# Rotary embeddings in a layer of a hybrid encoder: the last step on two engines, or as accumulating transfers into DRAM

## The chip, the cores and the metric

The kernel runs on one core of a Trainium2 chip. A core has five engines, each with its own instruction queue that it works through in order: TensorE (PE in the profile; PEld is its weight load), VectorE (DVE), ScalarE (ACT), GpSimd (POOL) and SyncE (SP). SP and POOL also issue the transfers (DMA) that move data between DRAM and the on-chip memory SBUF. Engines wait for one another and for transfers by semaphores. The metric is the device time of one execution in microseconds (us); smaller is better.

## The reference

One layer on 1024 tokens of width 1024, in float32: a feed-forward block, a token mixer and a second feed-forward block. The change is in the mixer. It multiplies the normalised input by one wide matrix whose columns are split into retention queries, keys, values and gates and the inputs of a neighbourhood attention:

```python
def _rotary(x, pos):
    half = x.shape[-1] // 2
    inv = 1.0 / (ROPE_BASE ** jnp.linspace(0.0, 1.0, half, dtype=jnp.float32))
    ang = pos[:, None] * inv[None, :]
    cos, sin = jnp.cos(ang), jnp.sin(ang)
    x1, x2 = x[..., :half], x[..., half:]
    return jnp.concatenate([x1 * cos - x2 * sin, x1 * sin + x2 * cos], axis=-1)
...
rq, rk, rv, rg, nq, nk, nv, g_ret, g_na = jnp.split(u @ w_in, points, axis=-1)
q = _rotary(heads(rq, RET_QK_DIM), pos)
k = _rotary(heads(rk, RET_QK_DIM), pos) * (RET_QK_DIM ** -0.5)
```

There are four retention heads of 128 channels. The queries and keys of a head, 128 x 1024 numbers each, are rotated: the first 64 channels of every token are mixed with the last 64.

## The kernel before

All products are formed with three matmuls on operands split into a high and a low part. `split` (L61, L62) makes them: ACT rounds a weight tile to the high part `wh`, DVE subtracts and so makes the low part `wl`. A matmul with `wl` (L90) can't start before DVE has done L62. The matmul lines are L88, L89 and L90.

The projections of the mixer are cut into jobs. One job yields two output tiles of 128 channels by 1024 tokens, by Winograd's scheme with seven products instead of eight (`Pairs.run`, L494 to L536). A product is a chain of twelve matmuls into one PSUM bank of 128 x 512. TensorE forms them in the order a11, s2, a12, s3, s1, a22, s4. DVE and ACT add the results into four quarters in SBUF: L509 (ACT), L514, L517, L524, L527, L528, L532 and L535 (DVE). The quarters are numbered j = 0 to 3; j // 2 says which of the two tiles, j % 2 which half of the tokens. They are finished in the order 0, 3, 1, 2, the first after the third product (L517), the second after the fifth (L527), then one after each of the last two (L532, L535). DVE also forms the next job's combined weights (L510, L511, L521, L530) and splits them.

When a quarter is done, `done(j)` handles it. Of the jobs around the change, four are rotary jobs (queries and keys of one head) and behind each stands a job of gates that ACT passes through silu (L1353); two jobs with a sigmoid follow. In a rotary job `rotate` (L1030 to L1033) turns each quarter in SBUF with four elementwise instructions: the two halves are multiplied crosswise with the sine table into a second tile `t`, the quarter is multiplied with the cosine table, and the two are added. Quarters 0 and 2 are turned by POOL, quarters 1 and 3 by DVE. Then `store` (L68) writes the quarter to DRAM from POOL's queue: to `rq` for queries, to `rk` for keys. They are read much later, by the retention.

Quarters and second tiles share six buffers of 128 x 512, named `ev`, and so do the quarters of the other jobs. A buffer is used again when its last reader is done, a store among them.

The order on each engine is not the order of the program. A scheduler lists the instructions engine by engine with its own estimate of times, picks a free buffer for each tile and puts in the waits. On the chip every engine keeps that order.

Of the kernel before, what the change touches and what calls it, by code (L numbers as in the profile page):

```python
# [13 lines left out]
ALU = mybir.AluOpType  # L14
# [1010 lines left out]
            nc.vector.tensor_scalar(q, q, RET_SCALE, None, ALU.mult)  # L1025


def rotate(eng, t, x, cos, sin):

    eng.tensor_tensor(t[0:64], x[64:128], sin[64:128], ALU.mult)  # L1030
    eng.tensor_tensor(t[64:128], x[0:64], sin[0:64], ALU.mult)
    eng.tensor_tensor(x, x, cos, ALU.mult)
    eng.tensor_tensor(x, x, t, ALU.add)  # L1033


def ret_cores(c, pool, spool, d, dec, fill, n):
# [157 lines left out]
def trunk_layer(ctx: ExitStack, tc, x, xt, g1a, w1i, w1o, g1b, gma, wmt, wnv, wrv, logits, dtab, rope, bias,  # L1194
                wro, wno, wmo, gmb, g2a, w2i, w2o, g2b, out):
    nc = tc.nc
# [5 lines left out]
    c = Core(tc, const, wpool, psum, dram)  # L1202
# [21 lines left out]
    def pool(stack, name, side="left"):  # L1224
        return stack.enter_context(tc.tile_pool(name=name, bufs=1, side=side, reuse_waits="tile"))
# [49 lines left out]
    def vproj(src, groups, done):  # L1275

        for toks in groups:
            banks = {t: c.bank() for t in toks}
            for k in range(KT):
                if k % 2 == 0:  # L1280
                    w = ahead.pop(k // 2) if k // 2 in ahead else c.load_w(src[k // 2])
                for t in toks:
                    tt = slice((t % 4) * P, (t % 4 + 1) * P)
                    c.mm3(banks[t], [q[:, k % 4, tt] for q in xh(t // 4, k // 4)], w[k % 2], k == 0, k == KT - 1)
                    yield
            for t in toks:
                done(t, banks[t])
# [32 lines left out]
    for f, k in zip(rest, FLIP_FILL):  # L1320
        fill(k)
        f = f()
# [5 lines left out]
    with tc.tile_pool(name="pa", bufs=1, reuse_waits="tile") as pa:  # L1328
        evpool[:] = [pa]
        fill.drain()  # L1330
        turners = (nc.gpsimd, nc.vector, nc.gpsimd, nc.vector)

        def half():
            return pa.tile([P, 512], F32, tag="ev", name="ev", bufs=6)

        tabs = [[pa.tile([P, 512], F32, tag="tab", name="tab", bufs=4) for _ in range(2)] for _ in range(2)]
        for h in range(2):
            for j in range(2):
                nc.sync.dma_start(tabs[h][j], rope[:, j, h * 512:(h + 1) * 512])

        for i, (_, _, f, g, fn) in enumerate(jobs):
            parts = {}

            def part(j):
                parts[j] = half()
                return parts[j]

            def done(j):
                h = j % 2
                if fn == "rotary":  # L1350
                    rotate(turners[j], half(), parts[j], *tabs[h])
                elif fn is not None:
                    nc.scalar.activation(parts[j], parts[j], fn)  # L1353
                c.store((f, g)[j // 2][:, h * 512:(h + 1) * 512], parts[j])
            mx.run(i, part, done)
            if i == 2:
                x1pool = pool(x1_stack, "x1b", "right")
                a21[:] = [x1pool.tile([P, 4, 512], F32R, name=f"a21{q}") for q in "hl"]
                for k in range(2):
                    raw = c.raw(d["a21"][:, 2 * k:2 * k + 2].rearrange("p k t -> p (k t)"))  # L1360
                    c.split(*[q[:, 2 * k:2 * k + 2].rearrange("p k t -> p (k t)") for q in a21], raw)
            if i == NHP - 1:
                for _ in vproj(wnv, ((4, 5, 6, 7),), done_nv):
                    pass
                for cb in range(4):
                    nc.sync.dma_start(d["nvg"][cb].rearrange("t (r c) d -> (t r) c d", r=4),
                                      d["nv"][:, KEY_OFF[cb]:KEY_OFF[cb] + 32, :])
# [216 lines left out]
```

## Time and profile before

| | |
|---|---|
| time, median of 3 runs | 2288.16 us (2287.96 to 2288.34) |
| the profiled execution | span 2285.9 us; 2.3 us below the median of the runs, which time what lies around the span too |
| TensorE busy | 2210.8 us, 97% |
| DVE busy | 1686.3 us, 74% |
| ACT busy | 1000.7 us, 44% |
| POOL busy | 650.9 us, 28% |
| the four rotary jobs with the gate jobs behind them | 814.9 to 978.9 us |

A row of a group names line, engine, operation, output and inputs, shape and count, then busy time in us, the mean of one in ns, and the idle time of the engine before it with what ended it. A row in order of time gives start, duration and, in brackets, the idle time before it. A wait row reads "who waited <- for whom: us in total, times, longest". A window row gives the busy time of each engine in a stretch (from:to), then the granted TensorE clock (1.00 is full speed), the share of the DMA engines' time and GB/s. Times within the execution count from the start of the span.

### The profile page before, as it was taken

To read this page: it belongs to the slowest core of one execution; us is meant where nothing else is said; L and a number is where in the kernel's file an instruction comes from. 1 tells how busy PE (TensorE), PEld (TensorE's weight loads), DVE (VectorE), ACT (ScalarE), POOL (GpSimd) and SP (SyncE) were. 2 spreads that over 40 slices of the span, in tenths; PEclk is the share of its full clock that TensorE was granted. 3 is DMA by queue.
4 is the path that set the end of the run, shared out by engine and by line. 5 is a ranking of instruction groups with operands and counts; after the bars stand their busy time and mean duration, and the time that the engine had idled before them with its cause. 6 is when DMAs were issued, how large, how long until landed. Compare 5 with 4: busy or idle time off the path is not lost. (4 is left out here: it accounts for less than half of the span.)

```text
span 2285.9 us, 30140 instructions
## 1 busy us (share of the span) xinstructions
PE 2210.8 (97%) x10232; PEld 1828.4 (80%) x10232; DVE 1686.3 (74%) x2928; ACT 1000.7 (44%) x2086; POOL 650.9 (28%) x779
## 2 busy tenths in 40 slices
PE   6899999999998999999999999999899999999998
PEld 5688888888787887778888888887578888888886
DVE  7998878755568667969876678537988888886444
ACT  5444434332344322259875665315544343433232
POOL 1121212169424133401101222101531212125942
PEclk9999999999999999999999999999999999999999
DMA  6353434597555452357754566766434444349865
GB/s 248 134 193 134 175 129 175 213 379 282 203 178 172 149 184 79 111 187 255 219 165 165 166 212 233 288 219 206 171 133 171 166 150 163 140 144 369 303 224 181
DMA packets 150090, 444.11 MB, mean 194 GB/s; under 512 B 18800, under 2 KB 46576, under 8 KB 147824
## 3 DMA queue, kind: packets, MB, share of 16 engines
q1 hardware_dynamic: 111216, 314.23, 40.2%
q0 software_dynamic: 38720, 127.96, 14.6%
q8 instruction: 81, 1.33, 0.2%
q14 instruction: 73, 0.60, 0.1%
HBM read 305.80 MB, written 140.51 MB: 195 GB/s over the span
## 5 line engine op out<-in xcount | busy, mean ns | idle before, releaser
L62 DVE TENSOR_TENSOR wl<-wraw,wh 128x512 fp32r<-128x512 f32 x512 | 363.9, 730 | 83.1 <-ACT wh L61 82.3
L61 ACT CAST wh<-wraw 128x512 fp32r<-128x512 f32 x516 | 297.9, 618 | 213.5 <-DVE wraw L530 63.8
L88 PE MATMUL ps<-wh,g 128*128 128x512 f32 x484 | 188.7, 390 | 0.0
L89 PE MATMUL ps<-wl,g 128*128 128x512 f32 x484 | 188.5, 389 | 0.0
L90 PE MATMUL ps<-wh,g 128*128 128x512 f32 x484 | 188.3, 389 | 0.0
L552 ACT ACTIVATE c<-c 128x512 f32<-128x512 f32 x88 | 55.5, 632 | 205.8 <-DVE c L517 105.8
L62 DVE TENSOR_TENSOR wl<-w,wh 128x512 fp32r<-128x512 f32 x77 | 75.5, 993 | 84.9 <-ACT wh L61 83.9
L62 DVE TENSOR_TENSOR wl<-x,wh 128x512 fp32r<-128x512 f32 x77 | 80.5, 1066 | 75.8 <-ACT wh L61 74.8
L61 ACT CAST wh<-t 128x512 fp32r<-128x512 f32 x58 | 36.0, 621 | 191.1 <-DVE t L511 191.0
L88 PE MATMUL ps<-a11h,wh 128*128 128x512 f32 x276 | 111.7, 405 | 7.5 <-ACT wh L61 7.3
L90 PE MATMUL ps<-a11h,wl 128*128 128x512 f32 x276 | 109.7, 398 | 5.0 <-DVE wl L62 4.9
L88 PE MATMUL ps<-a22h,wh 128*128 128x512 f32 x280 | 109.9, 392 | 0.0
L90 PE MATMUL ps<-a22h,wl 128*128 128x512 f32 x280 | 109.2, 390 | 0.6 <-DVE wl L62 0.6
L89 PE MATMUL ps<-a11l,wh 128*128 128x512 f32 x276 | 109.5, 397 | 0.1
L88 PE MATMUL ps<-a12h,wh 128*128 128x512 f32 x276 | 108.9, 394 | 0.3 <-ACT wh L61 0.3
L90 PE MATMUL ps<-a12h,wl 128*128 128x512 f32 x276 | 107.9, 391 | 1.3 <-DVE wl L62 1.3
L89 PE MATMUL ps<-a22l,wh 128*128 128x512 f32 x280 | 109.1, 390 | 0.0
L89 PE MATMUL ps<-a12l,wh 128*128 128x512 f32 x276 | 107.7, 390 | 0.0
L89 PEld LDWEIGHTS ps<-wl,g 128*128 128x128 f32 x484 | 90.9, 188 | 18.9 <-DVE wl L62 0.5
L90 PEld LDWEIGHTS ps<-wh,g 128*128 128x128 f32 x484 | 90.8, 188 | 18.9
L88 PEld LDWEIGHTS ps<-wh,g 128*128 128x128 f32 x484 | 90.8, 188 | 18.9
L68 POOL DMA_DIRECT2D g0a<-gth x33 | 18.0, 550 | 290.9 <-ACT gth L599 273.8
(435 smaller groups left out, 6540.1 us busy)
## 6 DMA issues: line engine op xcount, KB each, us to landing
wraw<-in_dram SPq DMA_DIRECT2D x218, 512.0 KB, 4.4
g<-g0s SPq DMA_DIRECT2D x44, 512.0 KB, 4.2
g<-g1s SPq DMA_DIRECT2D x44, 512.0 KB, 4.6
g<-g0a SPq DMA_DIRECT2D x33, 512.0 KB, 3.2
g<-g1a SPq DMA_DIRECT2D x33, 512.0 KB, 4.4
g0s<-gth POOLq DMA_DIRECT2D x44, 256.0 KB, 4.4
g0s<-cmb POOLq DMA_DIRECT2D x44, 256.0 KB, 3.7
g1s<-gth POOLq DMA_DIRECT2D x44, 256.0 KB, 4.5
```

What stands on the lines that cost most here:

```text
L61: self.done = [nc.scalar.copy(h, src).ins, (eng or nc.vector).tensor_tensor(l, src, hf, ALU.subtract).ins]
L62: (eng or nc.vector).tensor_tensor(l, src, hf, ALU.subtract).ins]
L68: self.nc.gpsimd.dma_start(dst, src)
L88: mm(ps, a[0], b[0], start=start, stop=False)
L89: mm(ps, a[0], b[1], start=False, stop=False)
L90: mm(ps, a[1], b[0], start=False, stop=stop)
L552: nc.scalar.activation(gate[j], gate[j], AF.Silu)
```

## The change

A quarter is no longer finished in SBUF. DVE makes two multiplications over all 128 channels: the second tile `t` is the quarter times the sine table, in its own place, and the quarter is multiplied with the cosine table. The quarter is stored so. Then two transfers from POOL's queue add `t` into the stored tile in DRAM, each 64 rows: the lower half of `t` onto the upper half of the tile and the other way round. Such an accumulating transfer must wait until the store before it has landed, and until it has itself landed the buffer of `t` is held. The program calls these transfers (`swaps`) when the next quarter is done. What is stored in the end is the same sum.

```diff
-def rotate(eng, t, x, cos, sin):
-
-    eng.tensor_tensor(t[0:64], x[64:128], sin[64:128], ALU.mult)
-    eng.tensor_tensor(t[64:128], x[0:64], sin[0:64], ALU.mult)
-    eng.tensor_tensor(x, x, cos, ALU.mult)
-    eng.tensor_tensor(x, x, t, ALU.add)
+def rotate(c, t, x, cos, sin, dst):
+
+    tt = c.nc.vector.tensor_tensor
+    tt(t, x, sin, ALU.mult)
+    tt(x, x, cos, ALU.mult)
+    c.store(dst, x)
+
+    def swap():
+        c.nc.gpsimd.dma_start(dst[0:64], t[64:128], accum_op=ALU.add)
+        c.nc.gpsimd.dma_start(dst[64:128], t[0:64], accum_op=ALU.add)
+    return swap
...
-        turners = (nc.gpsimd, nc.vector, nc.gpsimd, nc.vector)
+        swaps = []
...
             def done(j):
                 h = j % 2
+                dst = (f, g)[j // 2][:, h * 512:(h + 1) * 512]
+                while swaps:
+                    swaps.pop()()
                 if fn == "rotary":
-                    rotate(turners[j], half(), parts[j], *tabs[h])
-                elif fn is not None:
+                    swaps.append(rotate(c, half(), parts[j], *tabs[h], dst))
+                    return
+                if fn is not None:
                     nc.scalar.activation(parts[j], parts[j], fn)
-                c.store((f, g)[j // 2][:, h * 512:(h + 1) * 512], parts[j])
+                c.store(dst, parts[j])
```

In the changed kernel the lines below the function stand a few lower, and L1031 and L1032 are the two multiplications, L1036 and L1037 the two accumulating transfers. ACT, SP and TensorE keep their order; DVE and POOL change in the four rotary jobs alone.

The following rows show the order on an engine, as built: line, operation, output and inputs, shape, and what it waits for (DMASW0 to DMASW7 are the semaphores that POOL's transfers take in turn; a number behind a name tells tiles of one kind apart). First DVE in the second rotary job, from L528 to the first split of the gate job behind it. Before:

```order
L528 TENSOR_TENSOR ev_7125<-ps_7191,ev_7125 128x512
L1030 TENSOR_TENSOR ev_7211<-ev_7208,tab_6142 64x512 [waits DMASW5_49,DVE_49]
L1031 TENSOR_TENSOR ev_7211<-ev_7208,tab_6142 64x512
L1032 TENSOR_TENSOR ev_7208<-ev_7208,tab_6141 128x512 [waits DVE_49]
L532 TENSOR_TENSOR ev_7189<-ps_7218,ev_7189 128x512 [waits PE_49]
L1033 TENSOR_TENSOR ev_7208<-ev_7208,ev_7211 128x512 [waits DVE_49]
L1030 TENSOR_TENSOR ev_7236<-ev_7189,tab_6142 64x512 [waits DMASW2_49,DVE_49,Pool_49]
L1031 TENSOR_TENSOR ev_7236<-ev_7189,tab_6142 64x512
L535 TENSOR_TENSOR ev_7125<-ps_7242,ev_7125 128x512 [waits PE_49]
L1032 TENSOR_TENSOR ev_7189<-ev_7189,tab_6141 128x512 [waits DVE_49]
L1033 TENSOR_TENSOR ev_7189<-ev_7189,ev_7236 128x512 [waits DVE_49]
L62 TENSOR_TENSOR wl_7273<-wraw_7266,wh_7272 128x512 [waits DMAHW2_49,Activation_49]
```

And now:

```order
L528 TENSOR_TENSOR ev_7125<-ps_7189,ev_7125 128x512
L1031 TENSOR_TENSOR ev_7211<-ev_7206,tab_6142 128x512 [waits DMASW5_49,DVE_49]
L1032 TENSOR_TENSOR ev_7206<-ev_7206,tab_6141 128x512 [waits DVE_49]
L532 TENSOR_TENSOR ev_7187<-ps_7216,ev_7187 128x512 [waits PE_49]
L1031 TENSOR_TENSOR ev_7236<-ev_7187,tab_6142 128x512 [waits DMASW6_49,DVE_49]
L1032 TENSOR_TENSOR ev_7187<-ev_7187,tab_6141 128x512 [waits DVE_49]
L535 TENSOR_TENSOR ev_7125<-ps_7240,ev_7125 128x512 [waits PE_49]
L1031 TENSOR_TENSOR ev_7260<-ev_7125,tab_6140 128x512 [waits DMASW7_49,DMASW0_49,DVE_49]
L1032 TENSOR_TENSOR ev_7125<-ev_7125,tab_6139 128x512 [waits DVE_49]
L62 TENSOR_TENSOR wl_7271<-wraw_7264,wh_7270 128x512 [waits DMAHW2_49,Activation_49]
```

Six rows of rotation stand between L528 and L62 where eight stood. The first of the last two, which writes the second tile of quarter 2 (`ev_7260`), now waits for DMASW7 and DMASW0, the two accumulating transfers of quarter 0.

DVE in the first rotary job, from L527 on. Before:

```order
L527 TENSOR_TENSOR ev_6896<-ps_6879,ev_6877 128x512 [waits DMASW6_49,DMASW4_49,PE_49]
L528 TENSOR_TENSOR ev_6813<-ps_6879,ev_6813 128x512
L1030 TENSOR_TENSOR ev_6899<-ev_6896,tab_6142 64x512 [waits DMASW7_49,DMASW5_49,DVE_49]
L1031 TENSOR_TENSOR ev_6899<-ev_6896,tab_6142 64x512
L532 TENSOR_TENSOR ev_6877<-ps_6906,ev_6877 128x512 [waits PE_49]
L1032 TENSOR_TENSOR ev_6896<-ev_6896,tab_6141 128x512 [waits DVE_49]
L1030 TENSOR_TENSOR ev_6924<-ev_6877,tab_6142 64x512 [waits DMASW2_49,DVE_49,Pool_49]
L1033 TENSOR_TENSOR ev_6896<-ev_6896,ev_6899 128x512 [waits DVE_49]
L1031 TENSOR_TENSOR ev_6924<-ev_6877,tab_6142 64x512
L535 TENSOR_TENSOR ev_6813<-ps_6930,ev_6813 128x512 [waits PE_49]
L1032 TENSOR_TENSOR ev_6877<-ev_6877,tab_6141 128x512 [waits DVE_49]
L62 TENSOR_TENSOR wl_7001<-wraw_6954,wh_7000 128x512 [waits Activation_49]
```

And now:

```order
L527 TENSOR_TENSOR ev_6894<-ps_6877,ev_6875 128x512 [waits DMASW6_49,DMASW4_49,PE_49]
L528 TENSOR_TENSOR ev_6813<-ps_6877,ev_6813 128x512
L1031 TENSOR_TENSOR ev_6899<-ev_6894,tab_6142 128x512 [waits DMASW7_49,DMASW5_49,DVE_49]
L62 TENSOR_TENSOR wl_6999<-wraw_6952,wh_6998 128x512 [waits Activation_49]
L1032 TENSOR_TENSOR ev_6894<-ev_6894,tab_6141 128x512 [waits DVE_49]
L532 TENSOR_TENSOR ev_6875<-ps_6904,ev_6875 128x512 [waits PE_49]
L62 TENSOR_TENSOR wl_7022<-wraw_6954,wh_7021 128x512 [waits Activation_49]
L1031 TENSOR_TENSOR ev_6924<-ev_6875,tab_6142 128x512 [waits DMASW6_49,DVE_49]
L535 TENSOR_TENSOR ev_6813<-ps_6928,ev_6813 128x512 [waits PE_49]
L1032 TENSOR_TENSOR ev_6875<-ev_6875,tab_6141 128x512 [waits DVE_49]
L1031 TENSOR_TENSOR ev_6948<-ev_6813,tab_6140 128x512 [waits DMASW7_49,DMASW0_49,DVE_49]
L62 TENSOR_TENSOR wl_7041<-wraw_6952,wh_7040 128x512 [waits Activation_49]
```

The splits of the gate job's weights (L62) move forward: two of them stand ahead of the last two quarters' rotation and the third ahead of its last row, where the first stood behind seven rows of rotation. The quarter that POOL turned comes to DVE, with the wait for DMASW7 and DMASW0.

POOL in the second rotary job. Before:

```order
L1030 TENSOR_TENSOR ev_7165<-ev_7124,tab_6140 64x512 [waits DMASW2_49,DVE_49]
L1031 TENSOR_TENSOR ev_7165<-ev_7124,tab_6140 64x512
L1032 TENSOR_TENSOR ev_7124<-ev_7124,tab_6139 128x512 [waits DMASW0_49,Pool_49]
L1033 TENSOR_TENSOR ev_7124<-ev_7124,ev_7165 128x512 [waits Pool_49]
L68 DMA rq_99<-ev_7124 128x512 [waits Pool_49]
L68 DMA rk_100<-ev_7208 128x512 [waits DMASW7_49,DVE_49]
L1030 TENSOR_TENSOR ev_7260<-ev_7125,tab_6140 64x512 [waits DMASW6_49,DVE_49]
L1031 TENSOR_TENSOR ev_7260<-ev_7125,tab_6140 64x512
L1032 TENSOR_TENSOR ev_7125<-ev_7125,tab_6139 128x512 [waits DMASW1_49,Pool_49]
L68 DMA rq_99<-ev_7189 128x512 [waits DVE_49]
L1033 TENSOR_TENSOR ev_7125<-ev_7125,ev_7260 128x512 [waits Pool_49]
L68 DMA rk_100<-ev_7125 128x512 [waits Pool_49]
```

And now:

```order
L68 DMA rq_99<-ev_7124 128x512 [waits DMASW6_49,DVE_49]
L1036 DMA rq_99<-ev_7165 64x512 [waits DMASW7_49,DMASW6_49]
L1037 DMA rq_99<-ev_7165 64x512 [waits DMASW0_49]
L68 DMA rk_100<-ev_7206 128x512 [waits DMASW1_49,DVE_49]
L68 DMA rq_99<-ev_7187 128x512 [waits DMASW2_49,DVE_49]
L1036 DMA rk_100<-ev_7211 64x512 [waits DMASW3_49,DMASW1_49]
L1037 DMA rk_100<-ev_7211 64x512 [waits DMASW4_49]
L1036 DMA rq_99<-ev_7236 64x512 [waits DMASW5_49,DMASW2_49]
L1037 DMA rq_99<-ev_7236 64x512
L68 DMA rk_100<-ev_7125 128x512 [waits DMASW7_49,DVE_49]
L1036 DMA rk_100<-ev_7260 64x512 [waits DMASW7_49,DMASW0_49]
L1037 DMA rk_100<-ev_7260 64x512
```

The eight elementwise rows are gone, and behind each store come two rows L1036 and L1037, the first of which waits for that store to land. The stores of the later quarters stand behind them in the queue; quarter 1's store was put ahead of quarter 3's accumulations.

## The prediction

> **What bounds the kernel now.** I read the page's first part, then the stage that holds the change in windows, then who waited for whom there, then the engines in order of time.
>
> ```profile
> PE 2210.8 (97%) x10232; PEld 1828.4 (80%) x10232; DVE 1686.3 (74%) x2928; ACT 1000.7 (44%) x2086; POOL 650.9 (28%) x779
> ```
>
> TensorE is busy 97% of 2285.9 us, so an edit on other engines can only win stretches where TensorE waits. The four windows below run from the start of one L517 (product a12 added up in a rotary job) to the same line two jobs later: one rotary job and the silu job behind it, called a pair here.
>
> ```profile
> core 0: us, PE busy (x) PEld busy (x) DVE busy (x) ACT busy (x) POOL busy (x), PEclk, DMA share, GB/s
> 814.92:854.41 39.49, 38.67 (x169) 31.38 (x168) 33.64 (x44) 11.19 (x20) 16.73 (x16) 1.00 0.50 176
> 854.41:899.92 45.51, 40.62 (x169) 32.82 (x168) 32.83 (x45) 11.10 (x20) 15.69 (x16) 0.92 0.30 102
> 899.92:939.41 39.49, 38.67 (x169) 31.38 (x168) 34.24 (x45) 11.19 (x20) 16.77 (x16) 1.00 0.29 103
> 939.41:978.91 39.50, 38.69 (x169) 31.38 (x168) 34.23 (x45) 12.47 (x21) 16.77 (x16) 1.00 0.29 103
> ```
>
> Here are VectorE's (DVE's) instructions of the second pair, in order of time: start, duration, and the idle time before.
>
> ```profile
> 854.41 0.69 DVE L517 TENSOR_TENSOR ev<-ps,ev 128x512 f32<-128x512 f32 x1 [1.97 <-PE ps L90]
> 857.13 0.69 DVE L524 TENSOR_TENSOR ev<-ps,ev 128x512 f32<-128x512 f32 x1 [2.03 <-PE ps L90]
> 859.85 0.69 DVE L527 TENSOR_TENSOR ev<-ps,ev 128x512 f32<-128x512 f32 x1 [2.03 <-PE ps L90]
> 860.46 0.68 DVE L528 TENSOR_TENSOR ev<-ps,ev 128x512 f32<-128x512 f32 x1
> 861.15 0.69 DVE L1030 TENSOR_TENSOR ev<-ev,tab 64x512 f32<-64x512 f32 x1
> ...
> 867.23 1.64 DVE L1033 TENSOR_TENSOR ev<-ev 128x512 f32<-128x512 f32 x1
> 868.79 1.75 DVE L62 TENSOR_TENSOR wl<-wraw,wh 128x512 fp32r<-128x512 f32 x1
> ```
>
> L517, L524 and L527 each wait for one product of TensorE and stand 2.72 us apart, so a product costs 2.72 us and a pair of 14 products 38.08. The windows exceed that by 1.41, 7.43, 1.41 and 1.42 us, 11.67 in all. That is the most the change can win here. Who takes it:
>
> ```profile
> PE ps L90 <- DVE wl L62: 7.3, 7, 4.9
> ...
> 832.09 0.50 PE L90 MATMUL ps<-a12h,wl 128*128 128x512 f32 x1 [0.43 <-DVE wl L62]
> 835.49 0.50 PE L90 MATMUL ps<-s3h,wl 128*128 128x512 f32 x1 [0.39 <-DVE wl L62]
> ...
> 870.60 0.80 PE L90 MATMUL ps<-a11h,wl 128*128 128x512 f32 x1 [4.89 <-DVE wl L62]
> ```
>
> All of TensorE's idle time from 806 to 982 us has one cause: the low part `wl` of a weight tile of the next job, which DVE makes too late. In the first, third and fourth pair it is two short stalls, in the second one long one.
>
> **Why DVE is late.** First pair, DVE and then POOL in order of time, and last the group of the stage's eight L62 that split a computed tile `t` (count, busy us, mean ns, idle before):
>
> ```profile
> 830.25 1.79 DVE L62 TENSOR_TENSOR wl<-wraw,wh 128x512 fp32r<-128x512 f32 x1
> 831.96 1.77 DVE L1033 TENSOR_TENSOR ev<-ev 128x512 f32<-128x512 f32 x1
> 833.65 3.48 DVE L62 TENSOR_TENSOR wl<-wraw,wh 128x512 fp32r<-128x512 f32 x2
> ...
> 829.82 1.67 POOL L1030 TENSOR_TENSOR ev<-ev,tab 64x512 f32<-64x512 f32 x1 [0.67 <-DVE ev L535]
> ...
> L62 DVE TENSOR_TENSOR wl<-t,wh 128x512 fp32r<-128x512 f32 x8 | 5.5, 688 | 0.6
> ```
>
> While POOL rotates its second quarter (four instructions from 829.82 on), an L62 that takes 0.69 us elsewhere takes 1.74 to 1.79. Two DVE quarters of four instructions stand ahead of it.
>
> **The change part by part.**
>
> *Arithmetic.* Per rotary job before: two quarters of 4 instructions on DVE, two of 4 on POOL. After: four quarters of 2 on DVE, none on POOL. Half-height and full-height ones cost the same, by the rows of the stage:
>
> ```profile
> L1030 DVE TENSOR_TENSOR ev<-ev,tab 64x512 f32<-64x512 f32 x8 | 5.5, 687 | 0.2
> L1032 DVE TENSOR_TENSOR ev<-ev,tab 128x512 f32<-128x512 f32 x8 | 5.5, 683 | 0.0
> L1032 POOL TENSOR_TENSOR ev<-ev,tab 128x512 f32<-128x512 f32 x8 | 12.7, 1589 | 0.6
> L1033 POOL TENSOR_TENSOR ev<-ev 128x512 f32<-128x512 f32 x8 | 12.3, 1538 | 0.6
> L1030 POOL TENSOR_TENSOR ev<-ev,tab 64x512 f32<-64x512 f32 x8 | 11.8, 1472 | 24.7 <-DVE ev L517 21.3 <-DVE ev L535 3.4
> L1031 POOL TENSOR_TENSOR ev<-ev,tab 64x512 f32<-64x512 f32 x8 | 11.7, 1461 | 0.5
> ```
>
> So DVE's count stays at 8 a job, but two of them move to the first quarter, where DVE sat idle about 2 us per product (rows L524, L527), and the last three quarters cost 6 instructions in place of 8. POOL's 32 instructions (12.7 + 12.3 + 11.8 + 11.7 = 48.5 us) go, and with them the slowed DVE instructions.
>
> *First, third and fourth pair.* With 0.69 in place of 1.79, and two of the next job's three splits now standing ahead of the last two rotations (the order of the first pair above), the split for a12 is ready some 8 us before its matmul. The stalls go: 1.41 + 1.41 + 1.42 = 4.24 us.
>
> *Second pair.* Here all rotations still stand ahead of the split that TensorE waits for, so I walk the new order with the old pace: 0.61 us from start to start where an instruction doesn't need the one before, 0.70 where it does. L527 at 859.85, L528 860.46, the j3 quarter 861.15 and 861.76; L532 waits for the next product, 859.85 + 2.72 = 862.57; j1 quarter 863.25 and 863.95; L535 waits for the last product, 865.29; j2 quarter 865.98 and 866.6; L62 from 867.3 to 868.0, and TensorE goes on at 868.05 instead of 870.60: 2.55 us won. TensorE's last matmul ended at 870.60 - 4.89 = 865.71 and the next was due at about 865.55 (matmuls start 0.227 us apart, each shown for 0.39), so the loss falls from 5.05 to 2.5. The rest of the 7.43, 2.38 us, is the half clock that followed.
>
> *The clock.* Its rows: TensorE after idle stretches of about 3 us, and windows with the granted clock in the third column from the right.
>
> ```profile
> 730.28 0.47 PE L88 MATMUL ps<-s1h,wh 128*128 128x512 f32 x1 [3.02 <-DVE ev L520]
> 1022.63 0.44 PE L909 MATMUL ps<-k,qh 128*128 128x384 f32 x1 [2.51 <-ACT qh L64]
> 1613.03 1.22 PE L89 MATMUL ps<-wl,gh 128*128 128x512 f32 x2 [3.03 <-DVE wl L62]
> ...
> 726.00:734.00 8.00, 4.97 (x22) 3.80 (x21) 6.89 (x11) 3.63 (x8) 1.29 (x1) 1.00 0.38 131
> 1018.00:1026.00 8.00, 5.49 (x25) 4.15 (x24) 6.34 (x19) 5.29 (x11) 0.00 (x0) 1.00 0.97 274
> 1613.00:1623.00 10.00, 8.23 (x21) 5.21 (x21) 9.25 (x12) 3.04 (x6) 5.14 (x5) 0.51 0.46 158
> 869.00:875.00 6.00, 4.41 (x10) 3.31 (x11) 5.79 (x5) 0.84 (x2) 4.98 (x5) 0.50 0.13 48
> ```
>
> 4.89 us idle halved the clock, 2.51 didn't, and of two gaps of 3.0 one did. The forecast gap is 868.05 - 865.71 = 2.34, below the one that went free, so I take the 2.38 as won; lost, it is the lower end. The Trainium skill ("TensorE: Matmul & The Clock Gate", section "Why this matters for your kernels") wants no gaps over about 3 us, and says (section "Part 1: The HAM clock gate") that the window of 3.4 us is free-running. By that the sum is the same, the split pair of 3.0 us gaps agrees, and a gap of 2.34 wouldn't fill a window.
>
> *The transfers.* Added: 32 accumulating transfers of 64 rows (128 KB), on POOL's queue. Each first one of a quarter waits on POOL for its quarter's store to land; behind it stand later stores. The trace has none that accumulates. Nearest rows (issue, size, us to landing), and one store on POOL:
>
> ```profile
> 860.87 0.58 POOL L68 DMA_DIRECT2D rq<-ev  x1 [0.30 <-POOL ev L1033]
> ...
> rg<-rg SPq DMA_DIRECT2D x32, 128.0 KB, 2.5
> ...
> rq<-ev POOLq DMA_DIRECT2D x8, 256.0 KB, 2.3
> ...
> nvg<-nv SPq DMA_DIRECT2D x4, 9.3
> ...
> DMA to landing us min/median/max: 2.9/4.5/12.6
> ```
>
> An accumulation reads and writes DRAM: at least a store's 2.3 us, and at most the 12.6 of the slowest transfer on `nvg`, which is copied from DRAM to DRAM (median 9.3). I take a load and a store one after the other, 2.5 + 2.3 = 4.8, since these move tiles of this size between the same two places.
>
> Who needs them: six `ev` buffers serve four quarters and their products, so the j2 quarter's product reuses the j0 product's buffer (second pair's order: L1031 waits for DMASW7 and DMASW0). In the second pair j0 is done at 856.5, its store issues at 856.8 and lands at 859.1, the two accumulations issue at 859.4 and 860.0. DVE wants the buffer at 865.98: 6.0 us after the second issue, against 4.8. Hidden, with 1.2 to spare. In the first pair the same walk from L517 brings DVE to j2 at about 827, and the split behind it is wanted by the fifth product of the silu job, 814.92 + 8 x 2.72 + 0.45 = 837.1; so j2 may start as late as 835.7, while the second accumulation issues at about 820.5: 15.2 us of room. The silu job's own buffers wait for the j3 accumulations, issued near 828; their reader, L514, only frees PSUM, of which six banks stand ready. The load on POOL (12 transfers a job at 0.58) is less than the rotations that leave. ACT and SP keep their order; 8 MB more traffic in a stage whose DMA share is 0.29 to 0.50 costs nothing.
>
> *Sum.* 4.24 + 2.55 + 2.38 = 9.2 us of the profiled 2285.9. The three runs have a median of 2288.16, 2.3 us above that span; taking 9.2 off gives 2279.0. TensorE runs in order, so what follows moves with it.
>
> **Rivals.**
>
> *The clock drops all the same* after the 2.34 us gap: 2.38 given back, 2281.4. For it: one 3.03 gap that did. Against: 2.51 that didn't.
>
> *The two halves run one after the other*, 9.6 us from the first issue at 859.4 to 869.0. Then j2 starts 3.0 later, TensorE resumes at 871.05, 0.45 behind before, with the half clock: 4.24 - 0.45 = 3.8 won, 2284.4, no measurable change (0.2%, 4.6 us, is about what can be told from none). For it: nothing in the trace, which has no two halves of one tile. The Trainium skill ("DMA: Bandwidth & Descriptors", section "Rules for kernel authors") says that two transfers to disjoint partition halves serialize; no run here shows it.
>
> *Slower: the accumulation lands late and stands in front of TensorE.* Its place is the j2 quarter of the second pair: each us beyond 6.0 costs one, and soon the half clock's 2.38. At 12.8 us from issue the 9.2 less the clock's 2.4 are gone, at 15.2 the other three pairs start to lose too, and from some 16 the kernel is measurably slower. At 20 us: the second pair resumes at 882.05, 11.45 late, the others lose 20 - 15.2 - 1.41 = 3.4 each, in all 21.6, 2309.8. For it: 12.6 was seen on DRAM copies. Against: those moved under a DMA load that the second pair lacks (0.30).
>
> *Given back later:* the stretch of half clock at 1613 to 1623 follows a gap of 3.03 us and can shift with the earlier arrival. Up to 4 us either way (8.23 us of TensorE work at 0.51); 2283 or 2275.
>
> **How the numbers follow.** Forecast 0.60, clock drop 0.10, halves in turn 0.10, late landing 0.15, given back later 0.05. The range reaches from the forecast with 4 us won at 1613 (2275.0, rounded down to 2274.5) past the halves in turn to a landing at the seen 12.6 us (2279.0 + 6.6 + 2.4 = 2288.0); the lower bound of 2.3 us changes nothing, since 4.8 is hidden already. It leaves out most of the slower case and little else. Faster: forecast, clock drop and half of the last, 0.72; same: halves in turn and the rest, 0.13; slower 0.15.
>
> **What would show it.** Right: the four windows near 38.1, 40.6, 38.1, 38.1; all L62 near 0.69; TensorE idle in the stage once, for 2.3 us; accumulations landing in 3 to 6 us. Wrong: DVE idle ahead of L1031 with a DMA as the cause, a clock of 0.5 behind it, or POOL's stores of `rg` issued late.

## The result, and the profile after

The changed kernel takes 2281.1 us (median of 7 runs, 2278.7 to 2286.2), the kernel before 2288.3 on the same chip (7 runs, 2287.7 to 2293.4). The ratio is 0.9964, with a 95% interval of 0.9950 to 0.9977: 0.36% faster, 7.2 us by the medians and 8.2 by the ratio. The profiled execution took 2281.1 us; its span is 2279.3, 6.6 below that of before.

The page's first part and then the windows of the four pairs, from L517 to L517 as in the prediction (columns: TensorE, its weight load, DVE, ACT and POOL busy, granted clock, DMA share, GB/s):

```profile
PE 2209.3 (97%) x10232; PEld 1830.4 (80%) x10232; DVE 1662.9 (73%) x2928; ACT 1000.5 (44%) x2086; POOL 629.9 (28%) x779
```

```profile
818.39:856.47 38.08, 38.08 (x169) 31.53 (x168) 27.10 (x43) 11.09 (x20) 11.37 (x16) 1.00 0.73 206
856.47:897.42 40.95, 38.56 (x169) 31.37 (x168) 28.95 (x45) 11.10 (x20) 11.38 (x16) 1.00 0.52 143
897.42:935.50 38.08, 38.08 (x169) 31.53 (x168) 27.62 (x44) 11.21 (x20) 11.43 (x16) 1.00 0.50 138
935.50:973.58 38.08, 38.08 (x169) 31.53 (x168) 27.62 (x44) 12.49 (x21) 11.39 (x16) 1.00 0.52 139
```

Three pairs are at the 38.08 of pure TensorE work. The second keeps 2.87, at full clock. The four sum to 155.19 where they were 163.99: 8.80 won. Over the execution DVE has as many instructions as before (2928) and is busy 23.4 us less (1662.9, before 1686.3); in the stage it is 111.3 us where it was 134.9. TensorE's waits in the stage, then DVE in the second pair from the last product on, then DVE's split in the stage's groups:

```profile
PE ps L90 <- DVE wl L62: 2.4, 1, 2.4
```

```profile
867.35 0.69 DVE L535 TENSOR_TENSOR ev<-ps,ev 128x512 f32<-128x512 f32 x1 [0.57 <-PE ps L90]
868.08 0.69 DVE L1031 TENSOR_TENSOR ev<-ev,tab 128x512 f32<-128x512 f32 x1
868.80 0.69 DVE L1032 TENSOR_TENSOR ev<-ev,tab 128x512 f32<-128x512 f32 x1
869.41 0.69 DVE L62 TENSOR_TENSOR wl<-wraw,wh 128x512 fp32r<-128x512 f32 x1
...
L62 DVE TENSOR_TENSOR wl<-wraw,wh 128x512 fp32r<-128x512 f32 x54 | 35.5, 685 | 9.7 <-ACT wh L61 9.7
```

Of the seven stalls one is left. The j2 quarter's multiplication (868.08) has no idle time ahead of it, so the transfers that it must wait for had landed. Every L62 is at 0.69; before, the group of 49 had a mean of 908 ns.

The transfers, from the groups, DVE's waits and the DMA issues of the stage:

```profile
L1036 POOL DMA_DIRECT2D rq<-ev x8 | 7.0, 875 | 23.4 <-DMA rq<-ev 23.3
L1037 POOL DMA_DIRECT2D rq<-ev x8 | 9.2, 1154 | 0.0
...
DVE ev L1031 <- DMA rq<-ev: 5.4, 2, 3.4
DVE ev L514 <- DMA rk<-ev: 2.2, 2, 1.4
...
rq<-ev POOLq DMA_DIRECT2D x16, 128.0 KB, 4.3
rk<-ev POOLq DMA_DIRECT2D x16, 128.0 KB, 3.7
```

An accumulating transfer of 64 rows lands 3.7 to 4.3 us after its issue. DVE does wait for transfers, stores among them, 7.6 us in all, in the first and the fourth pair. None of it reaches TensorE.

Over the whole execution the stage gives 8.80 and the profile shows 6.6. The stage begins 3.47 later than before (818.39 against 814.92), although the orders of DVE and TensorE ahead of it are the same in both kernels; behind it 1.27 is won. Of the 3.47, 2.1 are there by 720 us and 1.4 come between 730 and 734, where the same gap of 3.0 us that went free before (730.28 in the prediction's rows) halved the clock:

```profile
732.38 0.77 PE L88 MATMUL ps<-s1h,wh 128*128 128x512 f32 x1 [3.00 <-DVE ev L520]
...
731.89:735.30 3.41, 2.92 (x7) 2.37 (x8) 3.27 (x6) 0.86 (x2) 0.00 (x0) 0.50 0.91 306
```

The 1.27 is the sum of several steps of both signs. In the profiles below the stage begins anywhere from 814.7 to 820.8, in no relation to the edits.

### The profile page after: what moved, and what is told of

Its sections match the earlier page's. It is cut to its first block, busy times and chain, and to the rows that moved or that the text cites. A ratio compares the mean times of both kernels' runs of the same rounds, so it can differ in the third digit from the quotient of the medians.

```text
span 2279.3 us, 30175 instructions
## 1 busy us (share of the span) xinstructions
PE 2209.3 (97%) x10232; PEld 1830.4 (80%) x10232; DVE 1662.9 (73%) x2928; ACT 1000.5 (44%) x2086; POOL 629.9 (28%) x779
## 5 line engine op out<-in xcount | busy, mean ns | idle before, releaser
L62 DVE TENSOR_TENSOR wl<-wraw,wh 128x512 fp32r<-128x512 f32 x512 | 353.3, 708 | 85.4 <-ACT wh L61 84.7
L62 DVE TENSOR_TENSOR wl<-w,wh 128x512 fp32r<-128x512 f32 x77 | 76.4, 1005 | 84.2 <-ACT wh L61 83.2
L62 DVE TENSOR_TENSOR wl<-x,wh 128x512 fp32r<-128x512 f32 x77 | 78.8, 1040 | 76.5 <-ACT wh L61 75.1
L88 PE MATMUL ps<-s2h,wh 128*128 128x512 f32 x232 | 91.8, 396 | 6.8 <-ACT wh L61 6.8
```

The costliest lines, as they stand in the source:

```text
L62: (eng or nc.vector).tensor_tensor(l, src, hf, ALU.subtract).ins]
L88: mm(ps, a[0], b[0], start=start, stop=False)
```

## Experiments

All windows are cut like the ones above; where a row of L517 slipped in DVE's order, work moves from one window to the next, so the sum of the stage is the surest column.

| | pair 1 | pair 2 | pair 3 | pair 4 | stage | TensorE's longest stall |
|---|---|---|---|---|---|---|
| before | 39.49 | 45.51 | 39.49 | 39.50 | 163.99 | 4.89 |
| changed | 38.08 | 40.95 | 38.08 | 38.08 | 155.19 | 2.39 |
| e1 POOL's quarters left out | 38.07 | 42.89 | 38.08 | 38.08 | 157.12 | 2.89 |
| e2 all on DVE | 39.32 | 46.62 | 39.33 | 39.33 | 164.60 | 5.77 |
| e3 no accumulation | 38.09 | 40.93 | 38.08 | 38.08 | 155.18 | 2.4 |
| e4 multiplied on POOL | 38.32 | 41.07 | 38.02 | 38.08 | 155.49 | 1.61 |
| e5 changed, again | 38.08 | 40.92 | 38.08 | 38.07 | 155.15 | 2.38 |
| e6 j2 one step later | 38.60 | 38.95 | 38.08 | 38.08 | 153.71 | 0.93 |
| e7 accumulated twice | 42.54 | 46.24 | 38.08 | 38.08 | 164.94 | 8.69 |
| e8 one transfer of 128 rows | 42.84 | 44.94 | 38.08 | 38.08 | 163.94 | 3.71 |
| e9 j0 twice | 39.25 | 45.80 | 38.08 | 38.08 | 161.21 | 5.16 |
| e10 j0 three times | 40.42 | 50.88 | 38.08 | 38.08 | 167.46 | 10.09 |

**Is it POOL's work beside DVE, or the number of DVE's instructions?** The theory: POOL's elementwise work slows DVE, and its removal is the whole gain. The rival: what counts is two instructions fewer ahead of the split. e1 takes POOL's work away and leaves the rest of the kernel before:

```diff
                 if fn == "rotary":
-                    rotate(turners[j], half(), parts[j], *tabs[h])
+                    if turners[j] is nc.vector:
+                        rotate(turners[j], half(), parts[j], *tabs[h])
```

> The kernel before, with the two quarters that POOL turns left unturned (their rotation is left out, they are stored as they are). DVE keeps its 8 rotation instructions a job, 4 a quarter, nothing accumulates in DRAM. Theory, contention: all the gain comes from POOL's elementwise work being gone from beside DVE. Walking the order of DVE's instructions from L517 on at 0.61 and 0.70 us, the split that TensorE waits for in the second pair is ready at the same place as in the changed kernel to within 0.1 us. Expected: the four pairs at 38.1, 41.0, 38.1, 38.1; one stall of TensorE in the stage, 2.4 to 2.5 us; every L62 near 0.69 us. Rival, count: the gain comes from DVE having two instructions fewer ahead of the split in the late quarters; then the pairs keep 39 to 39.5 and the second stays above 43. End to end the theory gives what the changed kernel has, about 2280 to 2282, the rival about 2286 to 2288.

Time 2281.3 us (10 runs), ratio to before 0.9961 (0.9947 to 0.9974). DVE's L535 in the second pair, TensorE's only stall in the stage, and a window of 2 us behind it:

```profile
867.91 0.69 DVE L535 TENSOR_TENSOR ev<-ps,ev 128x512 f32<-128x512 f32 x1
...
870.59 0.50 PE L90 MATMUL ps<-a11h,wl 128*128 128x512 f32 x1 [2.89 <-DVE wl L62]
...
872.50:874.50 2.00, 2.00 (x6) 1.56 (x5) 1.86 (x4) 2.00 (x5) 0.00 (x0) 0.50 0.00 0
```

DVE's order in the stage is that of the kernel before, instruction for instruction, and its busy time there is 112.1 us and not 134.9. Three pairs come to 38.08, so there the removal of POOL's work is enough by itself. In the second pair the theory falls short by 1.9 us. The split stands behind as many instructions after L535 as in the changed kernel, but L535 itself is no longer held by TensorE (no idle time in its row): the two more instructions ahead of it cost 0.50 us. That lengthened TensorE's gap from 2.39 to 2.89, and behind this one the clock halved: the other 1.44. So 6.87 of the 8.80 are POOL's work and 1.93 are the shorter order, most of that by way of the clock.

**What if DVE simply does it all?** e2 is the kernel before with one line changed:

```diff
-        turners = (nc.gpsimd, nc.vector, nc.gpsimd, nc.vector)
+        turners = (nc.vector,) * 4
```

> The kernel before with all four quarters turned on DVE in four instructions each, nothing on POOL and nothing accumulated: 16 rotation instructions a job in place of 8. Theory, contention plus place: without POOL beside it DVE has room in three pairs, which come to 38.1; in the second pair six rotation instructions and not two stand between L535 and the split that TensorE waits for, four more of about 0.62, so TensorE resumes 2.4 us later than in the changed kernel, a gap of 4.9 us, which halves the clock as the gap of 4.89 did before (2.4 more): second pair 45 to 46, stage about 160, so 5 longer than the changed kernel and 4 shorter than before. Rival, count: with twice the instructions on DVE all pairs grow past the kernel before, to 40 or more each.

Time 2292.7 us (10 runs), ratio to before 1.0021 (1.0007 to 1.0034): a little slower, where the theory had 4 us faster.

```profile
831.06 0.50 PE L90 MATMUL ps<-s2h,wl 128*128 128x512 f32 x1 [0.95 <-DVE wl L62]
871.13 0.79 PE L90 MATMUL ps<-a11h,wl 128*128 128x512 f32 x1 [5.77 <-DVE wl L62]
```

The second pair's gap is 5.77 and not 4.9, and the other three pairs stall once each for 0.95 on the split for s2, which now stands behind the rotations; the forecast had no stall there. Neither theory had it whole: the pairs didn't grow past 40, as pure count would have it. Taking the work off POOL is worth nothing if DVE gets all of it back. It is the transfers, which add and also cross the halves, that make the room: DVE has 8 rotation instructions a job and not 16. With 12 (e8 below, where the transfer adds and DVE crosses) the stage is back at 163.94.

**Do the transfers cost anything?** e3 leaves them out:

```diff
     def swap():
-        c.nc.gpsimd.dma_start(dst[0:64], t[64:128], accum_op=ALU.add)
-        c.nc.gpsimd.dma_start(dst[64:128], t[0:64], accum_op=ALU.add)
+        pass
```

> The changed kernel without the accumulating transfers (the sine part of the rotation is left out of the result). Theory, hidden transfers: the stage stays as it is with them, 38.1, 40.9, 38.1, 38.1, to within 0.2 us each; the waits of DVE for the transfers on rq and rk (5.4 and 2.2 us in the changed kernel) go, and TensorE gains nothing from it. Rival, the transfers cost: the second pair falls by more than 0.5 us or the first pair's stage changes.

The stage takes 155.18 against 155.19, each pair within 0.02. (Its single run took 2284.8 us, above the changed kernel's median: the difference lies outside the stage, as above.) The transfers are hidden. DVE's waits for transfers shrink from 7.6 to 0.7 us, and TensorE gains nothing by it.

**Contention put back, in the changed kernel.** e4 multiplies quarters 0 and 2 on POOL:

```diff
-def rotate(c, t, x, cos, sin, dst):
+def rotate(c, eng, t, x, cos, sin, dst):

-    tt = c.nc.vector.tensor_tensor
+    tt = eng.tensor_tensor
...
-                    swaps.append(rotate(c, half(), parts[j], *tabs[h], dst))
+                    swaps.append(rotate(c, (nc.gpsimd, nc.vector)[j % 2], half(), parts[j], *tabs[h], dst))
```

> The changed kernel with the two multiplications of quarters 0 and 2 on POOL in place of DVE; the accumulating transfers stay. Theory, contention: the L62 that run while POOL multiplies (two of 1.5 to 1.6 us after each of these quarters) take 1.7 to 1.8 us again, the others 0.69. In the second pair two DVE instructions less stand ahead of the split, 1.3 us, but it runs beside POOL and takes 1.1 longer: second pair 40.4 to 41, others 38.1 to 38.8. Rival, count: with DVE's load halved the second pair comes to 39.3 and no L62 is slow.

DVE, POOL and TensorE in the second pair, in order of time (L1031 and L1032 are the multiplications, L1036 and L1037 the transfers):

```profile
865.37 0.68 DVE L62 TENSOR_TENSOR wl<-wraw,wh 128x512 fp32r<-128x512 f32 x1
868.25 2.47 DVE L62 TENSOR_TENSOR wl<-t,wh 128x512 fp32r<-128x512 f32 x1
870.64 4.17 DVE L62 TENSOR_TENSOR wl<-wraw,wh 128x512 fp32r<-128x512 f32 x3
...
868.32 1.84 POOL L1031 TENSOR_TENSOR ev<-ev,tab 128x512 f32<-128x512 f32 x1
870.11 1.73 POOL L1037 DMA_DIRECT2D rq<-ev  x1
870.69 2.96 POOL L1032 TENSOR_TENSOR ev<-ev,tab 128x512 f32<-128x512 f32 x1
...
866.10 0.50 PE L90 MATMUL ps<-a11h,wl 128*128 128x512 f32 x1 [0.93 <-DVE wl L62]
870.77 0.50 PE L90 MATMUL ps<-s2h,wl 128*128 128x512 f32 x1 [1.61 <-DVE wl L62]
```

The windows are within 0.1 us of the forecast (41.07; 38.0 to 38.3), the path there isn't. The split for a11 now runs at 865.37, before POOL multiplies, in 0.68. The one that is slowed is the next, for s2: 2.47 us where it has 0.69 alone, more than the 1.8 expected. That is one long stall exchanged for two short ones. POOL's own rows of 1.84 and 2.96 are not a slowing of that size: each starts while the transfer ahead of it is still being issued (L1037 from 867.73 takes 1.14, to 868.87; the next from 870.11 takes 1.73, to 871.84). Counted from there they take 1.29 and 1.81, where POOL's undisturbed multiplications before take 1.29 and those beside DVE 1.6. So contention is real and large, but it costs only what stands behind a slowed instruction at that moment.

**A better place, and the changed kernel once more.** e5 is the changed kernel; e6 calls the rotation of j2 one step later:

```diff
                 while swaps:
                     swaps.pop()()
+                while late:
+                    swaps.append(rotate(c, half(), *late.pop()))
+                if fn == "rotary" and j == 2:
+                    late.append((parts[j], *tabs[h], dst))
+                    return
                 if fn == "rotary":
```

> The changed kernel once more, beside the next one on the same chip. The stage at 38.1, 40.9, 38.1, 38.1 as in its first profile; the time 2279 to 2286 us, since the two profiles differed by several us outside the stage.

> The changed kernel with the two multiplications of the last quarter (j2), its store and its transfers called one step later in the program, when the next job's first quarter is done; nothing else. DVE's order in the second pair then has the split for a11 right behind L535, ahead of both multiplications. Theory, place: TensorE's only stall in the stage falls from 2.39 to about 1.0 us (L535 waits for TensorE's last product itself, the split follows 0.61 later), the clock holds, the second pair comes to 39.5 and the others stay at 38.1: stage 153.7 to 153.9 and not 155.2. The time falls by about 1.4 us, less than the runs of one kernel spread, so end to end the ratio to the changed kernel can't be told from 1. Rival, buffers: the later quarter holds its two buffers longer, the next job waits for a transfer, and a pair grows by 1 us or more.

e5: 2281.8 us (12 runs), ratio to before 0.9968 (0.9957 to 0.9979). e6: 2281.9 us (7 runs), 0.9967 (0.9952 to 0.9983). In e6, the four windows' last row and the only stall:

```profile
sum 153.71, PE 152.78 PEld 126.00 DVE 111.60 ACT 45.72 POOL 45.94; mean PE 38.20 PEld 31.50 DVE 27.90 ACT 11.43 POOL 11.48
...
868.93 0.50 PE L90 MATMUL ps<-a11h,wl 128*128 128x512 f32 x1 [0.93 <-DVE wl L62]
```

The place theory holds to 0.1 us: the gap falls from 2.38 to 0.93 and the stage from 155.15 to 153.71 (a row of L517 slipped, so the first two pairs are compared together: 77.55, forecast 77.6). DVE waits up to 5.1 us for a transfer elsewhere, so the rival's waits are there, but they stop nobody. End to end the 1.4 us can't be seen, as expected.

**How late may a transfer land?** e7 doubles every accumulation:

```diff
+        for _ in range(2):
-        c.nc.gpsimd.dma_start(dst[0:64], t[64:128], accum_op=ALU.add)
-        c.nc.gpsimd.dma_start(dst[64:128], t[0:64], accum_op=ALU.add)
+            c.nc.gpsimd.dma_start(dst[0:64], t[64:128], accum_op=ALU.add)
+            c.nc.gpsimd.dma_start(dst[64:128], t[0:64], accum_op=ALU.add)
```

> The changed kernel with each pair of accumulating transfers issued twice (the sine part is added twice, so the result is another); the second two must wait for the first two to land, which doubles the time until the buffer of the j0 quarter comes free. Theory, as in the forecast: room in the second pair is 6.0 us from the second issue, and an accumulation lands about 3.9 after its issue, so the second two issue near 865.7 and 866.3 on the changed kernel's time axis and land near 870.5; DVE's j2 multiplication, at 868.1 in the changed kernel, starts about 2.4 late with the transfer as the cause, TensorE's gap grows from 2.4 to about 4.8, and the clock halves: second pair 44.9 to 45.8. The third and fourth pair, with 15.2 of room, stay at 38.1 or lose under 2, the first loses 0 to 6, since its transfers are already late. Rival, the transfers are hidden anyhow: all four pairs as in the changed kernel.

One run, 2289.8 us; stage 164.94. POOL and then DVE in the second pair (L1037 and L1038 are the transfers here):

```profile
856.25 0.54 POOL L68 DMA_DIRECT2D rg<-ev  x1 [0.60 <-ACT ev L1363]
...
869.29 0.82 POOL L1037 DMA_DIRECT2D rq<-ev  x1 [1.87 <-DMA rq<-ev]
869.83 0.88 POOL L68 DMA_DIRECT2D rk<-ev  x1
...
865.03 0.69 DVE L1031 TENSOR_TENSOR ev<-ev,tab 128x512 f32<-128x512 f32 x1 [1.57 <-DMA rg<-ev]
873.08 0.69 DVE L1031 TENSOR_TENSOR ev<-ev,tab 128x512 f32<-128x512 f32 x1 [3.98 <-DMA rk<-ev]
```

Dearer than forecast, and by another way. The scheduler gave j2 another buffer, which waits for a plain store of the j3 quarter (`rk`); that store was issued at 869.83 because it stood on POOL behind an accumulation that waited for the one before it. The wait at 865.03 is another matter: it is for the store of `rg` issued at 856.25, which took 8.7 us to land. So this run shows that POOL's queue passes a wait on, but it doesn't measure the room of 6.0 us. For that e9 and e10 repeat the accumulation of j0 alone and name the buffer (n is 2 in e9 and 3 in e10):

```diff
     def swap():
+        for _ in range(n):
...
+                    if j != 2:
+                        parts[j, "t"] = half()
-                    swaps.append(rotate(c, half(), parts[j], *tabs[h], dst))
+                    swaps.append(rotate(c, parts[0 if j == 2 else j, "t"], parts[j], *tabs[h], dst, 2 if j == 0 else 1))
```

> The changed kernel with the accumulation of the j0 quarter alone issued twice (its sine part is added twice, so the result is another) and the j2 quarter given the same tile t as j0 by name, so that the buffer in question is the one of the forecast; DVE's order in the second pair is that of the changed kernel. Theory, room of 6.0 us: on the changed kernel's time axis the first two issue at 861.5 and 862.1 and land about 3.5 and 4.0 later, the second two issue when these land, near 865.1 and 866.1, and land near 870.1; j2's multiplication, at 868.1 in the changed kernel, starts 2.0 late, TensorE's gap is 4.4, the clock halves: second pair 44.4 to 45.4, third and fourth 38.1, the first 38 to 42. Rival, the transfer never stands in front of TensorE: second pair 41.

> The same with the accumulation of j0 issued three times, each round waiting for the one before. Theory: one more landing of about 4 us, j2's multiplication 6.0 late, TensorE's gap 8.4: second pair 48.4 to 49.4, so 4.0 above the run with two rounds, one us for each us; the third and fourth pair, where 15.2 us of room were worked out and the last lands 12 after the second issue, stay at 38.1 though DVE waits for the transfer there. Rival: no step from two to three rounds.

The second transfer of the last two rounds of j0 on POOL, the j2 quarter on DVE and TensorE's stall, first in e9, then in e10:

```profile
861.24 1.16 POOL L1038 DMA_DIRECT2D rq<-ev  x1
...
865.59 1.13 POOL L1038 DMA_DIRECT2D rq<-ev  x1
...
869.61 0.69 DVE L1031 TENSOR_TENSOR ev<-ev,tab 128x512 f32<-128x512 f32 x1 [2.81 <-DMA rq<-ev]
...
871.68 0.79 PE L90 MATMUL ps<-a11h,wl 128*128 128x512 f32 x1 [5.16 <-DVE wl L62]
```

```profile
871.31 1.13 POOL L1038 DMA_DIRECT2D rq<-ev  x1
...
876.21 0.97 POOL L1038 DMA_DIRECT2D rq<-ev  x1
...
880.19 0.69 DVE L1031 TENSOR_TENSOR ev<-ev,tab 128x512 f32<-128x512 f32 x1 [7.74 <-DMA rk<-ev]
...
882.26 0.80 PE L90 MATMUL ps<-a11h,wl 128*128 128x512 f32 x1 [10.09 <-DVE wl L62]
```

In both, DVE goes on 4.0 us after the last issue (869.61 - 865.59 = 4.02; 880.19 - 876.21 = 3.98). From two rounds to three j2 starts 4.93 later, TensorE's gap is 4.93 longer and the second pair 5.08: one us for each, as forecast. The step is 4.93 and not 4.0: other issues stood between on POOL, and the second transfers of the last two rounds are 876.21 - 871.31 = 4.90 apart. The third and fourth pair stay at 38.08 even so. (The profile puts e10's wait down to `rk`; the instruction waits for transfers of j0 to `rq` alone.) In e9 j2 was 2.81 late and not 2.0: it could have started at 869.61 - 2.81 = 866.80, 5.6 after the first second issue at 861.24 and not 6.0, and the second round took 865.59 - 861.24 = 4.35 and not 4.0. So both second pairs are above what was expected, 45.80 for 44.4 to 45.4 and 50.88 for 48.4 to 49.4. No run gives j2 this buffer with a single round, so the room itself rests on e9 alone.

**One transfer in place of two.** e8 swaps the halves on DVE:

```diff
-    tt(t, x, sin, ALU.mult)
+    tt(t[0:64], x[64:128], sin[64:128], ALU.mult)
+    tt(t[64:128], x[0:64], sin[0:64], ALU.mult)
...
-        c.nc.gpsimd.dma_start(dst[0:64], t[64:128], accum_op=ALU.add)
-        c.nc.gpsimd.dma_start(dst[64:128], t[0:64], accum_op=ALU.add)
+        c.nc.gpsimd.dma_start(dst, t, accum_op=ALU.add)
```

> The changed kernel with the halves swapped on DVE (the sine product in two multiplications of 64 rows, so 3 instructions a quarter and 12 a job) and one accumulating transfer of 128 rows (256 KB) a quarter in place of two of 64. Theory, place and count: in the second pair three more instructions stand ahead of the split, of which L535's wait hides about half; TensorE resumes about 1.4 us later, after a gap of 3.8, and the clock halves: second pair 43.7 to 44.7, the others 38.1 to 38.5. If two halves of one tile move side by side, one transfer of both lands in about what a half takes now, 3.5 to 5 us; if the two halves run one after the other, a half alone takes about half of what the pair of them needs, and the whole lands in 7 us or more.

One run, 2291.3 us; stage 163.94, all of the gain lost. The landing times of the accumulations in the stage, of the changed kernel (L1036, then L1037) and then of e8:

```profile
DMA to landing us min/median/max: 2.9/3.5/5.4
DMA to landing us min/median/max: 3.5/4.4/5.5
```

```profile
DMA to landing us min/median/max: 3.7/4.2/8.1
...
837.71 0.79 PE L90 MATMUL ps<-a12h,wl 128*128 128x512 f32 x1 [2.93 <-DVE wl L62]
875.89 0.79 PE L90 MATMUL ps<-a11h,wl 128*128 128x512 f32 x1 [3.71 <-DVE wl L62]
```

One transfer of 256 KB takes 4.2 us, a half 3.5 to 4.4. So most of it is a fixed price, and the two halves overlap: the second, issued 0.6 after the first, has landed 4.9 after the first's issue in the median of the sixteen quarters. The second pair is close to the forecast (44.94, just above 43.7 to 44.7; gap 3.71). The first isn't: with three instructions a quarter the scheduler put all the next job's splits behind the j2 quarter there, which waits for late transfers, and a gap of 2.93 came up that halved the clock.

## Why the prediction was right, and where it was off

*The bound.* The prediction put all that could be won at 11.67 us of stalls on L62. The stage won 8.80; 2.87 are left, in one stall of 2.39 (2.34 forecast).

*First, third and fourth pair.* Forecast 4.24, measured 1.41 + 1.41 + 1.42 = 4.24. e1 shows that the absence of POOL's work is enough for it; e2 that this holds only while DVE isn't given that work back. The prediction named the slowed L62 and the earlier splits together and didn't part them; in e1 no split stands earlier, so the slowed instructions were the cause of these stalls.

*Second pair.* Forecast 2.55 + 2.38 = 4.93, measured 4.56. TensorE goes on at 870.15; the forecast's 868.05, moved by the 2.06 by which this L517 starts later, is 870.11. What was off is the sum behind it: the loss was worked out as 2.5 and is 2.87, since the first matmuls after the gap follow each other more slowly than 0.227 (870.15, then 870.49).

*The clock.* The forecast took 2.38 as won, because the gap of 2.34 lies below one of 2.51 that went free. It was won, in both profiles of the changed kernel, but the reason doesn't hold, and luck had a part in it. Ahead of the very matmul that had waited 2.51 (L909), a gap of 2.48 halved the clock in e6 (to 1016.04) and one of 2.12 in e1 (to 1018.79), while 3.02 at 730 in the kernel before had gone free. The Trainium skill ("TensorE: Matmul & The Clock Gate", section "Why this matters for your kernels") allows gaps up to about 3 us; here the gaps of 2.48 and 2.12 were already too long.

What tells the gaps apart is where they lie. In the profiles the half clock comes and goes on a grid of 3.413 us: in the changed kernel's it begins at 690.93, 731.89 and 1018.61, 12 and 84 steps apart. Here are single steps of such a grid (TensorE's busy time is the first number behind the comma), first the kernel before, then the changed kernel around 730 and in the second pair, then e6:

```profile
728.44:731.85 3.41, 1.57 (x7) 1.34 (x8) 3.27 (x6) 0.00 (x0) 0.00 (x0) 1.00 0.45 149
731.85:735.26 3.41, 3.41 (x17) 2.81 (x16) 3.41 (x7) 2.92 (x6) 0.56 (x1) 1.00 0.44 159
...
728.48:731.89 3.41, 0.90 (x4) 0.38 (x2) 2.81 (x4) 1.61 (x4) 1.28 (x1) 1.00 0.00 0
...
865.02:868.43 3.41, 2.75 (x13) 1.94 (x11) 2.73 (x5) 0.00 (x0) 1.55 (x3) 1.00 0.29 107
868.43:871.84 3.41, 1.69 (x7) 1.42 (x8) 3.31 (x6) 0.20 (x1) 3.31 (x5) 1.00 0.91 138
...
1012.76:1016.17 3.41, 0.93 (x5) 0.47 (x4) 3.25 (x6) 3.36 (x8) 0.00 (x0) 1.00 1.01 253
1016.17:1019.58 3.41, 3.41 (x9) 2.84 (x10) 2.59 (x10) 1.28 (x4) 0.00 (x0) 0.50 0.86 299
```

The gap of 3.02 before lay across an edge and left 3.41 - 1.57 = 1.84 us idle in its worst step; the clock held. The 3.00 of the changed kernel left 3.41 - 0.90 = 2.51 in one step, and the next, 731.89 to 735.30 above, ran at 0.50. So did the one behind e6's step with 2.48 idle. In the twelve profiles all 67 steps at full clock between 60 and 2270 us with 2.0 us or more of idle time were followed by half the clock; 16 of the 41 with 1.5 to 1.9 were. The gap of 2.39 in the second pair fell across the edge at 868.43, 0.66 on one side and 1.72 on the other. The same gap inside one step would have been of the size that always halved it. e1's longer gap left 1.99 in a step of its profile, and that was enough. So the chance of 0.10 for a clock drop was too small, and the 2.38 are as much the place of that edge as the length of the gap. The prediction's other argument, that such a gap wouldn't fill a window, fails as well: a step needn't be idle throughout.

*The transfers.* Landing was taken as 4.8 and is 3.7 to 4.3 in the median. Room in the second pair was put at 6.0 from the second issue: 868.08 - 862.07 = 6.01. e3 shows that hiding is complete, e9 and e10 that beyond the room each us costs one. Two prices were missed. A pair of accumulations holds POOL for 1.74 us (from 861.49 to 862.07 + 1.16 = 863.23; the second's row starts before the first is through), 0.87 each and not the 0.58 of a plain store; and in the first pair a store took 9.4 us to land beside the DRAM copies, so DVE waited 2.0 and 3.4 there. The 15.2 us of room, worked out for that pair, took it up.

*The rivals.* The halves don't run one after the other (e8). The Trainium skill ("DMA: Bandwidth & Descriptors", section "Rules for kernel authors") would have had one transfer in place of two; here the one transfer is a little quicker, 4.2 us where the pair takes 4.9 from the first issue, but the two halves do overlap, and the instructions that the one transfer needs on DVE cost the whole gain. Late landing is a real mechanism with the price that was given (e10, 12 us more than the changed kernel in the stage), but a landing of 4 us is far from it. "Given back later" happened in part: the start of the stage moved by 3.47, which the change can't have done, and what lies behind it by 1.27 the other way, which was not taken apart.

*The time.* 2279.0 forecast, 2281.1 measured. Of the 2.1 between them 0.37 is the second pair; the rest is of the size by which runs of one kernel differ (2278.7 to 2286.2), and in the profile 1.4 us come from the half clock at 732 alone.

## What to carry to other kernels

A busy share says little about an engine's worth: taking elementwise work off POOL made DVE 17% less busy in this stage with the same instructions in the same order (e1), because POOL's had slowed them. An accumulating transfer moves an addition off the engines at about 4 us of latency and 0.9 us of POOL's queue; in this stage it is free where the buffer isn't wanted for longer than that, and one us for one us beyond. And look at what stands directly ahead of the instruction that the bounding engine waits for: moving two instructions behind it (e6) won more of the last stall than any change of engine. A gap's length alone doesn't tell what it does to the clock: here it was the idle time within a step of 3.41 us.

## What the runs showed that was not expected

An instruction of 0.69 us on DVE took 2.47 beside POOL's in e4's second pair and 3.0 in its first (a split at 835.7). The Trainium skill ("SBUF — State Buffer", section "SBUF: two separate sides") describes an exclusive lock on a port that the two share, held for a whole instruction. The traces agree with one of the two being blocked until the other's instruction is over. In the stage of the kernel before, 22 DVE instructions took 1.64 to 1.82 us, and every one of them ended 0.55 us after one of POOL's: in the prediction's rows, 830.25 + 1.79 = 832.04 and 829.82 + 1.67 = 831.49. In e4's rows it is 868.25 + 2.47 = 870.72 and 868.32 + 1.84 = 870.16. Together the 22 took 23.4 us more than at 0.69, which is the whole fall of DVE's busy time over the execution. DVE instructions with an input from PSUM were not slowed: in the same stage six ran beside POOL's, in 0.68 to 0.69 us.

A transfer that moves half the bytes lands hardly sooner (3.5 to 4.4 us for 128 KB, 4.2 for 256 KB). And a scheduler's choice can undo a clean experiment: doubling a latency (e7) made it pick another buffer, so that the run measured a queue and not the latency.
